# A hybrid decoder layer on one core: attention scores as 128-row contractions with parts spread by DMA, HGRN's updates and outputs as single lists, the relative bias padded to 128 rows and columns

## The chip, the cores and the metric

The kernel runs on one core of a Trainium2 chip. The metric is the time of one execution in microseconds (us). TensorE (PE) does the matrix products, and its weight loads (PEld) overlap with them; VectorE (DVE), ScalarE (ACT) and GpSimd (POOL) do the elementwise work; SyncE (SP) issues the DMAs. Each engine works through its own list of instructions in order.

## The reference, cut to what matters

One layer on x of 512 positions by 1024 channels, all in float32. One input projection (1024 to 3584 columns) feeds four branches of 256 channels each and four gates:

```
proj = x @ w_in                       # qa ka va | us | qc fc ic | qd kd vd | four gates
A: softmax(q k^T / 8 + bias) v        # 4 heads of 64, causal
B: diagonal state space (S5) and a gated linear unit
C: HGRN2: S_t = diag(f_t) S_{t-1} + (1 - f_t) outer i_t ; o_t = S_t^T q_t   # 4 heads of 64, chunks of 64
D: softmax over dilated windows       # 4 heads of 64, done as one biased causal softmax
y = concat(A, B, C, D); y = rms_norm(y) * gain * silu(gates)
x = layer_norm(ALPHA * x + y @ w_out)
```

With 512 positions all earlier keys are reachable, so A and D are both written as a full causal attention with a bias table added to the scores. The bias table (8 heads) is made on the chip from a small product, `rel_bias` against a 0/1 matrix of distances.

## The kernel before, in words

**Precision.** Most products are made of three fast ones (fp32r): a value is split into a high part `h` and a low part `l`, and `h*h + l*h + h*l` is summed in PSUM. So each projection tile of 128 rows by 512 columns takes 8 contraction steps of 3 matmuls. Some products (transposes, HGRN, S5, the product of probabilities and values) are plain fp32; the profile shows a plain fp32 product as two MATMUL instructions.

**Order.** The instruction order is not written by hand. `Order` (lines 132 to 262) is a planner: each task is a Python generator that yields instructions, or lists of PE instructions that stay together. A task has a priority (lower goes first). Projections (`projections`, priority 92) and the output product (`out_partial`, 91, `out_final`, 90) are the filler for PE; everything else goes between them when the planner's clocks say that its inputs are there, with a margin of 1 us for PE.

**Buffers.** `Tok` takes tokens and `o.rel` gives them back; a task that finds no token waits, in the planner's order. `u` stands for `NU` = 34 work tiles of 4 KB per partition. The PSUM banks are `pj` (3, projections and output product), `sc` (2, scores), `pt` (2, transposes) and `sm` (1). `raw` (4) are landing buffers of the weights, `wh` (5) the split weights. The output weights (`out_weights`) take 2 `u` tiles for each of six k steps, and ask for 6 free ones (`2 + SPARE`) before they do; the order of k is 6, 7, 4, 5, 0, 1, 2, 3. Weight loads, relays and the final stores all go through SP's one queue, in the planner's order.

**Attention before.** `evac_qk` (line 1076) copies a projected tile of two heads (head 0 in partitions 0 to 63, head 1 in 64 to 127) into `qt[name, ct][:, 0]` (high) and `[:, 1]` (low). `attn_pair` (line 1139) takes two heads and both `sc` banks, and issues six matmuls of 64 contraction rows, the two heads in turn, each in its own half of the array:

```
for j, (x, y) in enumerate(((0, 0), (1, 0), (0, 1))) for h in range(2)
```

Then `attn_head` (line 1153) adds the bias from `TB` and takes the row maximum (DVE), the exponential (ACT), transposes the probabilities (PE, ACT or DVE), and `attn_pv` multiplies by the values in 64-column halves of the array. There are 2 branches, query tiles i = 3, 2, 1, 0 with n = (i + 1) * 128 keys, and 2 pairs: 16 pairs. Branch A waits for the HGRN state (`START`), D for its own projections.

**HGRN before.** The chunk states (lines 1014 to 1031) come in four lists of 4 (the last of 2) products of 64 rows; after each, ACT or DVE adds the update to the running state, in order. The outputs (lines 1040 to 1065) come in two lists, each with products of 64 output columns (state times query) and then of 64 by 64 (in-chunk scores times values).

**Bias before.** `bias` (line 506) multiplies two slices of one tile of 34 rows, `relct`: 8 columns of table against 512 and then 128 columns of distances.

Of the kernel before, what the change touches and what calls it, by code (L numbers as in the profile page):

```python
# [11 lines left out]
F32 = mybir.dt.float32  # L12
# [253 lines left out]
def build(ctx: ExitStack, tc: tile.TileContext, xT, xN, w_in, w_out, ln_g, ln_b,  # L266
# [15 lines left out]
    def u(shape, nm, dt=F32):  # L282
        return up.tile(shape, dt, tag="u", name=nm)
# [104 lines left out]
    def load_feed():  # L388
        yield Wait("begun")
        for n_, p in enumerate(pieces):  # L390
            if n_ == 4:
                yield Tok(u=3)
                for nm, sh, sl, src in (("bc", [128, 4, 8, 32], None, s5bc.rearrange("p (a j c) -> p a j c", a=4, j=8)),
                                        ("cst2", None, None, consts[:, 586:874]), ("relct", [34, 648], None, relc),
                                        ("glw", [128, 1024], None, consts[:, 74:586])):
                    t = CT[nm] = u(sh, nm) if sh else cst2
                    yield Q.dma_start(t[:, 0:512] if nm == "glw" else t, src)
                    o.done(nm)
                    o.cur["chain"] = 0.0
            yield Tok(raw=1)  # L400
            raw = raws[p] = wp.tile([128, 512], F32, tag="raw", name=f"wr{p[0]}_{p[1]}", bufs=NR)
            yield Q.dma_start(raw, w_in[GROUPS.index(p[0]), :, 2 * p[1]:2 * p[1] + 2].rearrange("p k c -> p (k c)"))
            o.events["raw", p] = o.cur["chain"]
            o.cur["chain"] = 0.0
# [101 lines left out]
    def bias():  # L506

        yield Wait("us")
        yield Wait("relct")
        yield Delay(1.0)  # L510
        yield Tok(u=1)
        relct, bsb = CT["relct"], u([8, 640], "bsb")
        for a, n in ((0, 512), (512, 128)):
            yield Tok(sm=1)
            pb = ps(f"pb{a}", "sm")
            yield [T.matmul(pb[0:8, 0:n], relct[:, 640:648], relct[:, a:a + n], start=True, stop=True)]
            yield A.activation(bsb[:, a:a + n], pb[0:8, 0:n], AF.Copy)
            o.rel("sm")
        yield Q.dma_start(scr, bsb.unsqueeze(1).to_broadcast([8, NCP, 640]))
        o.rel("u", 2)  # L520
        yield Wait("hgrn levels")
        TB = gp.tile([128, 8, S], F32, tag="g", name="TB")
        for ph in range(128 // NCP):
            src_ = bass.AP(scr.tensor, 127 - NCP * ph, [[639, NCP], [NCP * 640, 8], [1, 512]])
            yield Q.dma_start(TB[NCP * ph:NCP * ph + NCP], src_)
            o.cur["chain"] = o.clk["PE"] + 1.5
        o.cur["chain"] = o.dma + 2.0
        TBq["t"] = TB
        o.done("TB")
# [366 lines left out]
    def hgrn():  # L896
# [114 lines left out]
        ic = H["ic"]  # L1011
        yield Tok(u=2)
        hst = [u([128, 4, 2, 128], f"hst{i}") for i in range(2)]
        for c2 in range(4):
            yield Tok(sc=1, pt=1)
            pu = [ps(f"pu{c2}_{q}", ("sc", "pt")[q], (128, 2, 128)) for q in range(2)]
            yield [T.matmul(pu[q][:, a], kt[64 * q:64 * q + 64, a, c2],
                            ic[64 * q:64 * q + 64, c2, 128 * a:128 * a + 128], start=True, stop=True)
                   for a in range(2) for q in range(2) if 2 * c2 + q < 7]
            for q in range(2):  # L1020
                c = 2 * c2 + q
                if c < 7:
                    h_ = hst[c // 4][:, c % 4]
                    if c == 0:
                        yield A.activation(h_, pu[q], AF.Copy)
                    else:
                        for a in range(2):
                            yield V.scalar_tensor_tensor(h_[:, a], hs[c - 1][:, a], tot[:, a, c:c + 1], pu[q][:, a],
                                                         OP.mult, OP.add)
                    hs[c] = h_  # L1030
                o.rel(("sc", "pt")[q])
        o.rel("u")
        o.done("hgrn state")
        o.rel("pT")
# [2 lines left out]
            yield G.memset(t_[64:128, :, :, 0:64], 0.0)  # L1037
        yield Tok(u=1)
        yC = u([128, 4, W], "yC")
        for tp in range(2):  # L1040
            yield Tok(sm=1)
            po = ps(f"ho{tp}", "sm", (128, 2, W))

            ops, ops2, seen = [], [], set()
            for t2 in range(2):
                c2 = 2 * tp + t2
                for a in range(2):
                    for q in range(2):
                        c = 2 * c2 + q
                        rq = slice(64 * q, 64 * q + 64)  # L1050
                        ca = slice(128 * a, 128 * a + 128)
                        if c:
                            ops.append(T.matmul(po[rq, t2, ca], qc[:, a, 64 * c:64 * c + 64], hs[c - 1][:, a],
                                                start=q not in seen, stop=False, skip_group_check=True))
                            seen.add(q)
                    for h in range(2):
                        for q in range(2):
                            c = 2 * c2 + q
                            rq = slice(64 * q, 64 * q + 64)
                            cl = slice(128 * a + 64 * h, 128 * a + 64 * h + 64)  # L1060
                            ops2.append(T.matmul(po[rq, t2, cl], st[h][rq, a, c2], ic[rq, c2, cl],
                                                 start=False, stop=(t2 == a == h == 1), skip_group_check=True))
            yield ops + ops2
            yield A.activation(yC[:, 2 * tp:2 * tp + 2], po, AF.Copy, scale=0.125)
            o.rel("sm")
        o.rel("u", 6)
        yield from norm_branch(3, yC)

# [5 lines left out]
    def evac_qk(n, sc):  # L1076
        def f(ct, po):
            yield Tok(u=1)
            t = qt[n, ct] = u([128, 2, S], f"{n}{ct}", F32R)
            yield A.activation(t[:, 0], po, AF.Copy, scale=sc)  # L1080
            yield V.scalar_tensor_tensor(t[:, 1], po, sc, t[:, 0].bitcast(F32), OP.mult, OP.subtract)
        return f

    def evac_v(n):
        def f(tp, po):
# [50 lines left out]
    HP = 6.5  # L1136
    ATT = {}

    def attn_pair(br, i, a, no):

        q_, k_ = (("qa", "ka"), ("qd", "kd"))[br]
        n = (i + 1) * 128
        yield Wait(q_, k_, "TB", *([("sc", no - 2)] if no else []))
        yield Tok(sc=2)
        o.done(("sc", no))
        sc = [ps(f"sc{i}_{4 * br + 2 * a + h}", "sc") for h in range(2)]
        qs = slice(128 * i, 128 * i + 128)
        yield [T.matmul(sc[h][:, 0:n], qt[q_, a][ROWS[h], x, qs], qt[k_, a][ROWS[h], y, 0:n], start=j == 0, stop=j == 2)
               for j, (x, y) in enumerate(((0, 0), (1, 0), (0, 1))) for h in range(2)]
        for h in range(2):  # L1150
            o.add(attn_head(br, i, 2 * a + h, no + h, sc[h]), HP + (no + h) * 0.01, f"head {br} {i} {2 * a + h}")

    def attn_head(br, i, hd, no, sc):
        v_ = ("va", "vd")[br]
        n = (i + 1) * 128
        hg = 4 * br + hd
        if no:
            yield Wait(("nl", no - 1))
        yield Tok(nl=1)
# [23 lines left out]
    def attn_pv(br, i, pairs):  # L1183

        v_ = ("va", "vd")[br]
        yield Wait(v_, *[("P", br, i, 2 * a + h) for a in pairs for h in range(2)])
        if pairs[0] == 0:
            yield Tok(sm=1)
            ATT[br, i] = ps(f"po{i}_{br}", "sm", (128, 4, 128))
            o.done(("po", br, i))  # L1190
        yield Wait(("po", br, i))
        po = ATT[br, i]
        yield [T.matmul(po[64 * h:64 * h + 64, a], vt[v_][:, kt, 128 * a + 64 * h:128 * a + 64 * h + 64],
                        ATT[br, i, 2 * a + h][:, kt], start=(kt == 0), stop=(kt == i))
               for a in pairs for kt in range(i + 1) for h in range(2)]
        o.rel("pT", 2 * len(pairs))
        o.rel("head", 2 * len(pairs))
        if pairs[-1] == 1:
            o.add(attn_norm(br, i, po), 1, f"norm {br} {i}")
            if i == TILES[-1]:  # L1200
                o.rel("u", 5)

    def attn_norm(br, i, po):
        yield Tok(sqa=1, ya=1)
# [41 lines left out]
    def attention():  # L1246
        n = 0
        for br in range(2):
            yield Wait(*(("qa", "ka", START), ("qd", "kd"))[br])
            for i in TILES:  # L1250
                for a in range(2):
                    yield Tok(head=2)
                    o.add(attn_pair(br, i, a, n), HP + n * 0.01, f"pair {br} {i} {a}")
                    n += 2


    lnt = {}
# [194 lines left out]
```

## Time and profile before

| | |
|---|---|
| median of 3 runs | 292.11 us (291.78 to 292.79) |
| profiled execution | 292.68 us, of which 290.9 us from the first to the last instruction (the span) |
| PE busy | 279.9 us (96% of the span), 1966 matmuls |
| PE weight loads | 225.8 us (78%) |
| DVE, ACT, POOL busy | 211.3, 142.6, 23.5 us (73%, 49%, 8%) |
| mean granted clock of TensorE | 0.994 of full speed |
| DMA | 31.08 MB, mean 107 GB/s |

The profile is of one execution. A busy engine is counted from the start of an instruction to its modelled end, and matmuls overlap, so the length of a stretch of PE work is read from the chain of waits (start, duration, what), whose pieces join end to end, not by adding durations of single matmuls.

### The profile page before, as it was taken

What the parts mean: (1) busy time and instruction counts of PE and PEld (TensorE: products, weight loads), DVE (VectorE), ACT (ScalarE), POOL (GpSimd) and SP (SyncE); (2) the same over time, 40 slices, a digit from 0 to 9 for tenths busy, and PEclk for the clock granted to TensorE, in tenths of its full rate; (3) what the DMA queues carried; (4) which work ended last, traced back from release to release, by engine and by line L of the source; (5) the groups of instructions that cost most, each with busy time, mean ns of one, the idle gap of its engine ahead of it and who ended that gap; (6) DMA issues with size and microseconds to landing.
All of it is one profiled execution on the core that took longest, in us unless ns stands there. A gap on an engine that the chain in (4) does not pass through costs nothing.

```text
span 290.9 us, 5251 instructions
## 1 busy us (share of the span) xinstructions
PE 279.9 (96%) x1966; PEld 225.8 (78%) x1966; DVE 211.3 (73%) x507; ACT 142.6 (49%) x281; POOL 23.5 (8%) x30
## 2 busy tenths in 40 slices
PE   7999999999999999989999999999999999999990
PEld 3678679988779977768897787777979777777890
DVE  2877999999999979479642465866768765776565
ACT  4677661325353433064588588876367753221000
POOL 1110000000000001100130010014000101020201
PEclk9999999999999999999999999999999999999997
DMA  6966435521322599922112320132512690121011
GB/s 194 310 190 207 133 110 120 154 82 44 104 74 66 132 127 114 163 89 74 36 57 85 95 94 0 48 98 73 149 34 74 208 357 16 44 101 55 20 72 72
DMA packets 18741, 31.08 MB, mean 107 GB/s; under 512 B 2426, under 2 KB 5882, under 8 KB 18716
## 3 DMA queue, kind: packets, MB, share of 16 engines
q1 hardware_dynamic: 18716, 30.76, 38.3%
q8 instruction: 15, 0.25, 0.4%
q14 instruction: 10, 0.08, 0.1%
HBM read 27.27 MB, written 2.42 MB: 102 GB/s over the span
## 4 chain that ended last, share of the span: by engine, by line
PE 84%; DMA 7%; DVE 5%; issue 1%; SPq 1%; ACT 1%; DVEq 0%; ACTq 0%
PE out L229 16%; PE pj_g L229 12%; PE po L229 4%; PE pj_vd L229 4%; PE pj_ic L229 4%; PE pj_kd L229 4%; PE pj_va L229 4%; PE pj_qc L229 4%; PE pj_qd L229 4%; PE pj_ka L229 4%; PE pj_us L229 4%; DMA wrg<-in_w_in_dram 4%; PE pt L229 3%; PE sc L229 3%; PE pj_qa L229 2%; PE y L229 2%
## 5 line engine op out<-in xcount | busy, mean ns | idle before, releaser
L229 PE MATMUL pj_g<-xh,whg 128*128 128x512 f32 x64 | 26.9, 421 | 0.0
L229 PE MATMUL pj_g<-xh,wlg 128*128 128x512 f32 x64 | 25.1, 392 | 0.0
L229 PE MATMUL pj_g<-xl,whg 128*128 128x512 f32 x64 | 25.1, 392 | 0.0
L229 ACT ACT_TABLE_LOAD x18 | 23.1, 1283 | 2.4 <-PE glu L229 1.4
L229 DVE CUSTOM_DVE_ANT_0 nl<-sc,TB 128x512 f32<-128x512 f32 (+3 forms) x32 | 14.6, 485 | 9.2 <-PE sc L229 9.1
L229 ACT ACTIVATE whg<-wrg 128x512 fp32r<-128x512 f32 x16 | 10.1, 629 | 22.6 <-PE pj_g L229 8.8
L229 PE MATMUL out<-woh,yh 128*128 128x512 f32 (+1 forms) x54 | 21.1, 391 | 0.0
L229 ACT ACTIVATE nl<-nl,nm 128x512 f32<-128x512 f32 (+3 forms) x32 | 17.8, 556 | 6.3 <-DVE nm L229 6.1
L229 PE MATMUL out<-woh,yl 128*128 128x512 f32 (+1 forms) x54 | 19.9, 368 | 0.0
L229 PE MATMUL out<-wol,yh 128*128 128x512 f32 (+1 forms) x54 | 19.8, 367 | 0.0
L229 DVE TENSOR_TENSOR wlg<-wrg,whg 128x512 fp32r<-128x512 f32 x16 | 11.0, 689 | 9.0 <-ACT whg L229 8.8
L229 POOL TENSOR_TENSOR msa<-msa,mhalf 128x4 f32<-128x4 f32 x8 | 9.0, 1122 | 100.8 <-DVE msa L229 100.8
L229 DVE COPY pT<-pt 128x512 f32<-128x512 f32 (+3 forms) x16 | 7.8, 488 | 12.1 <-PE pt L229 12.1
L229 PEld LDWEIGHTS pj_g<-xh,whg 128*128 128x128 f32 x64 | 12.0, 188 | 3.9 <-issue 1.4
L229 ACT ACTIVATE yh<-z 128x256 fp32r<-128x256 f32 (+1 forms) x12 | 5.7, 486 | 18.8 <-DVE z L229 18.8
L229 PE MATMUL pt<-ident,nl 128*128 128x128 f32 x80 | 14.3, 278 | 0.0
L229 PEld LDWEIGHTS pj_g<-xh,wlg 128*128 128x128 f32 x64 | 12.0, 188 | 2.7
L229 PEld LDWEIGHTS pj_g<-xl,whg 128*128 128x128 f32 x64 | 12.1, 189 | 1.9
L229 PEld LDWEIGHTS out<-woh,yh 128*128 128x128 f32 x54 | 10.2, 190 | 2.4 <-issue 0.8
L229 PEld LDWEIGHTS pt<-ident,nl 128*128 128x128 f32 x80 | 9.7, 140 | 3.1 <-issue 1.3
L229 PEld LDWEIGHTS out<-woh,yl 128*128 128x128 f32 x54 | 10.2, 189 | 1.8
L229 ACT ACTIVATE pT<-pt 128x512 f32<-128x512 f32 (+3 forms) x16 | 7.0, 434 | 9.1 <-PE pt L229 9.0
(312 smaller groups left out, 818.6 us busy)
## 6 DMA issues: line engine op xcount, KB each, us to landing
wrg<-in_w_in_dram SPq DMA_DIRECT2D x16, 256.0 KB, 4.9
wro<-in_w_out_dram SPq DMA_DIRECT2D x16, 256.0 KB, 2.8
xr<-in_xT_dram SPq DMA_DIRECT2D x8, 256.0 KB, 4.6
TB<-scr SPq DMA_DIRECT2D x8, 256.0 KB, 11.3
xn<-in_xN_dram SPq DMA_DIRECT2D x4, 512.0 KB, 8.2
out_dram<-xn SPq DMA_DIRECT2D x7, 256.0 KB, 2.0
raw<-in_w_in_dram SPq DMA_DIRECT2D x8, 128.0 KB, 4.6
wrus<-in_w_in_dram SPq DMA_DIRECT2D x4, 256.0 KB, 4.2
```

Of the source, the lines that this page charges most:

```text
L229: getattr(self.engines[op.eng], op.name)(*op.a, **op.k)
```

## The change

1. `relct` becomes a tile of 128 by 768 that POOL sets to zero before the 34 by 648 table is loaded into its corner; both bias products now take 128 rows and 128 columns of it.
2. HGRN's seven chunk updates are issued as one list of PE instructions into four PSUM banks (both `sc` and both `pt`), and the updates of the state follow.
3. HGRN's outputs are one list, into one `sm` and one `pt` bank: first all products of 64 output columns, then all of 64 by 64.
4. A new task `by_head` follows each evacuation of q and k. With four DMAs from tile to tile it builds, per head, a key tile that holds the 64 rows of the head twice (both with the high and the low part), and for the queries one tile in which partitions 0 to 63 hold a head's high part and 64 to 127 its low part. One score is then two matmuls of 128 rows: (q high over q low) with k high, and with k low. `attn_pair` is gone; each head issues its own two matmuls.

```diff
-                                        ("cst2", None, None, consts[:, 586:874]), ("relct", [34, 648], None, relc),
+                                        ("cst2", None, None, consts[:, 586:874]), ("relct", [128, 768], None, relc),
...
+                    if nm == "relct":
+                        yield G.memset(t, 0.0)
+                    yield Q.dma_start(t[:, 0:512] if nm == "glw" else t[0:34, 0:648] if nm == "relct" else t, src)
...
-            yield [T.matmul(pb[0:8, 0:n], relct[:, 640:648], relct[:, a:a + n], start=True, stop=True)]
+            yield [T.matmul(pb[:, 0:n], relct[:, 640:768], relct[:, a:a + n], start=True, stop=True)]
...
-        for c2 in range(4):
-            yield Tok(sc=1, pt=1)
...
+        yield Tok(sc=2, pt=2)
+        pu = [[ps(f"pu{x}_{q}", ("sc", "pt")[q], (128, 2, 2, 128)) for x in range(2)] for q in range(2)]
+        yield [T.matmul(pu[q][c2 // 2][:, c2 % 2, a], kt[64 * q:64 * q + 64, a, c2],
+                        ic[64 * q:64 * q + 64, c2, 128 * a:128 * a + 128], start=True, stop=True)
+               for c2 in range(4) for a in range(2) for q in range(2) if 2 * c2 + q < 7]
+        for c in range(7):
+            h_, p_ = hst[c // 4][:, c % 4], pu[c % 2][c // 4][:, c // 2 % 2]
+            if c == 0:
+                yield A.activation(h_, p_, AF.Copy)
+            else:
+                for a in range(2):
+                    yield V.scalar_tensor_tensor(h_[:, a], hs[c - 1][:, a], tot[:, a, c:c + 1], p_[:, a], OP.mult, OP.add)
+            hs[c] = h_
+            if c in (2, 3, 5, 6):
+                o.rel(("sc", "pt")[c % 2])
...
+        yield Tok(sm=1, pt=1)
+        pos_ = [ps(f"ho{tp}", ("sm", "pt")[tp], (128, 2, W)) for tp in range(2)]
+
+        ops, ops2 = [], []
         for tp in range(2):
...
-            yield ops + ops2
-            yield A.activation(yC[:, 2 * tp:2 * tp + 2], po, AF.Copy, scale=0.125)
-            o.rel("sm")
+        yield ops + ops2
+        for tp in range(2):
+            yield A.activation(yC[:, 2 * tp:2 * tp + 2], pos_[tp], AF.Copy, scale=0.125)
+            o.rel(("sm", "pt")[tp])
...
+            o.add(by_head(n, ct, t, n[0] == "k"), 5.5, f"by head {n} {ct}")
...
+    def by_head(n, ct, t, keys):
+        yield Tok(u=1 + keys)
+        if keys:
+            d = [u([128, 2, S], f"{n}{ct}_{h}", F32R) for h in range(2)]
+        else:
+            d = u([128, 2, S], f"{n}{ct}h", F32R)
+        last = 0.0
+        for h in range(2):
+            for x in range(2):
+                c = o.cur["chain"]
+                if keys:
+                    yield Q.dma_start(d[h][ROWS[x]].bitcast(F32), t[ROWS[h]].bitcast(F32))
+                else:
+                    yield Q.dma_start(d[ROWS[x], h].bitcast(F32), t[ROWS[h], x].bitcast(F32))
+                o.cur["chain"], last = c, o.cur["chain"]
+        o.cur["chain"] = last
+        qt[n, ct] = d
+        o.rel("u")
+        o.done((n, ct))
...
-    def attn_pair(br, i, a, no):
...
-        yield [T.matmul(sc[h][:, 0:n], qt[q_, a][ROWS[h], x, qs], qt[k_, a][ROWS[h], y, 0:n], start=j == 0, stop=j == 2)
-               for j, (x, y) in enumerate(((0, 0), (1, 0), (0, 1))) for h in range(2)]
...
+    def attn_head(br, i, hd, no):
...
+        yield Wait((q_, a), (k_, a), "TB", *([("sc", no - 1)] if no else []))
+        yield Tok(sc=1)
+        o.done(("sc", no))
+        sc = ps(f"sc{i}_{hg}", "sc")
+        yield [T.matmul(sc[:, 0:n], qt[q_, a][:, h, 128 * i:128 * i + 128], qt[k_, a][h][:, x, 0:n], start=x == 0, stop=x == 1)
+               for x in range(2)]
...
             if i == TILES[-1]:
-                o.rel("u", 5)
+                o.rel("u", 7)
...
-                for a in range(2):
-                    yield Tok(head=2)
-                    o.add(attn_pair(br, i, a, n), HP + n * 0.01, f"pair {br} {i} {a}")
-                    n += 2
+                for hd in range(4):
+                    yield Tok(head=1)
+                    o.add(attn_head(br, i, hd, n), HP + n * 0.01, f"head {br} {i} {hd}")
+                    n += 1
```

## Rows read from the trace of the kernel before

**Rows 1.** The page: busy us (share of the span) and instructions of PE.

```profile
PE 279.9 (96%) x1966; PEld 225.8 (78%) x1966; DVE 211.3 (73%) x507; ACT 142.6 (49%) x281; POOL 23.5 (8%) x30
```

**Rows 2.** The page: the chain that ended last, share of the span by engine.

```profile
PE 84%; DMA 7%; DVE 5%; issue 1%; SPq 1%; ACT 1%; DVEq 0%; ACTq 0%
```

**Rows 3.** Windows: length, busy by engine (PE, PEld, DVE, ACT, POOL), clock, DMA, GB/s.

```profile
120.00:130.00 10.00, 8.69 (x48) 6.50 (x48) 5.04 (x15) 4.36 (x8) 1.04 (x2) 1.00 0.56 141
```

**Rows 4.** Chain of waits, branch D's scores: start, us, engine, tile, instructions.

```profile
216.28 0.44 PE pt L229 x4
216.72 0.89 PE sc L229 x6
...
219.68 1.44 PE pj_vd L229 x12
221.33 0.72 PE sc L229 x6
222.05 0.59 PE pt L229 x4
...
236.79 0.55 PE sc L229 x6
237.33 1.62 PE out L229 x6
...
239.28 1.39 PE out L229 x6
...
245.82 0.48 PE sc L229 x6
246.30 1.58 PE out L229 x6
```

**Rows 5.** Chain of waits, the bias, HGRN, S5 and the gated unit.

```profile
34.97 0.95 PE pb L229 x2
35.92 2.96 PE pj_qc L229 x12
...
98.90 2.75 PE pj_g L229 x12
...
104.37 0.65 PE pu L229 x8
105.02 2.95 PE pj_g L229 x12
...
133.06 2.10 PE ho L229 x44
...
143.57 2.68 PE y L229 x24
146.25 4.10 PE pj_g L229 x18
...
173.90 1.36 PE glu L229 x6
```

**Rows 6.** Timeline of ACT: evacuation of va's first half, and of kt's second.

```profile
95.62 0.60 ACT L229 ACTIVATE va<-pj_va 128x512 f32<-128x512 f32 x1 [0.81 <-PE pj_va L229]
...
102.13 0.60 ACT L229 ACTIVATE fc<-kt 128x512 f32<-128x512 f32 x1 [1.59 <-PE kt L229]
```

**Rows 7.** The page: DMA issues, count, KB each, median us to landing.

```profile
wro<-in_w_out_dram SPq DMA_DIRECT2D x16, 256.0 KB, 2.8
...
TB<-scr SPq DMA_DIRECT2D x8, 256.0 KB, 11.3
```

**Rows 8.** Timeline of DVE: second half of qd evacuated.

```profile
206.71 0.69 DVE L229 SCALAR_TENSOR_TENSOR qd<-pj_qd,qd 128x512 fp32r<-128x512 f32 x1 [0.64 <-ACT qd L229]
```

**Rows 9.** Timeline of SP's queue: output weights, LayerNorm constants.

```profile
204.84 5.25 SPq L229 DMA_DIRECT2D wro<-in_w_out_dram  x4
221.03 10.03 SPq L229 DMA_DIRECT2D wro<-in_w_out_dram  x8
231.11 0.42 SPq L229 DMA_DIRECT2D lng<-in_ln_g_dram  x1
```

More of the change, by code (lines that the diff above doesn't have):

```diff
@@ L393, in load_feed @@
                 for nm, sh, sl, src in (("bc", [128, 4, 8, 32], None, s5bc.rearrange("p (a j c) -> p a j c", a=4, j=8)),
-                                        ("cst2", None, None, consts[:, 586:874]), ("relct", [34, 648], None, relc),
+                                        ("cst2", None, None, consts[:, 586:874]), ("relct", [128, 768], None, relc),
                                         ("glw", [128, 1024], None, consts[:, 74:586])):
                     t = CT[nm] = u(sh, nm) if sh else cst2
-                    yield Q.dma_start(t[:, 0:512] if nm == "glw" else t, src)
+                    if nm == "relct":
+                        yield G.memset(t, 0.0)
+                    yield Q.dma_start(t[:, 0:512] if nm == "glw" else t[0:34, 0:648] if nm == "relct" else t, src)
                     o.done(nm)
@@ L1013, in hgrn @@
         hst = [u([128, 4, 2, 128], f"hst{i}") for i in range(2)]
-        for c2 in range(4):
-            yield Tok(sc=1, pt=1)
[L1016 to L1026, printed above, removed]
-                        for a in range(2):
[L1028 to L1031, printed above, removed]
+        yield Tok(sc=2, pt=2)
[13 more added lines that the diff above has]
+                o.rel(("sc", "pt")[c % 2])
         o.rel("u")
@@ L1039, in hgrn @@
         yC = u([128, 4, W], "yC")
+        yield Tok(sm=1, pt=1)
+        pos_ = [ps(f"ho{tp}", ("sm", "pt")[tp], (128, 2, W)) for tp in range(2)]
+        ops, ops2 = [], []
         for tp in range(2):
-            yield Tok(sm=1)
-            po = ps(f"ho{tp}", "sm", (128, 2, W))
-            ops, ops2, seen = [], [], set()
+            po, seen = pos_[tp], set()
             for t2 in range(2):
@@ L1057, in hgrn @@
                         for q in range(2):
-                            c = 2 * c2 + q
                             rq = slice(64 * q, 64 * q + 64)
@@ L1137, in build @@
     ATT = {}
-    def attn_pair(br, i, a, no):
+    def attn_head(br, i, hd, no):
         q_, k_ = (("qa", "ka"), ("qd", "kd"))[br]
[L1142 to L1147, printed above, removed]
-        yield [T.matmul(sc[h][:, 0:n], qt[q_, a][ROWS[h], x, qs], qt[k_, a][ROWS[h], y, 0:n], start=j == 0, stop=j == 2)
-               for j, (x, y) in enumerate(((0, 0), (1, 0), (0, 1))) for h in range(2)]
[L1150 to L1154, printed above, removed]
+        a, h = divmod(hd, 2)
         n = (i + 1) * 128
         hg = 4 * br + hd
+        yield Wait((q_, a), (k_, a), "TB", *([("sc", no - 1)] if no else []))
[4 more added lines that the diff above has]
+               for x in range(2)]
         if no:
@@ L1250, in attention @@
             for i in TILES:
-                for a in range(2):
-                    yield Tok(head=2)
-                    o.add(attn_pair(br, i, a, n), HP + n * 0.01, f"pair {br} {i} {a}")
-                    n += 2
+                for hd in range(4):
+                    yield Tok(head=1)
+                    o.add(attn_head(br, i, hd, n), HP + n * 0.01, f"head {br} {i} {hd}")
+                    n += 1
     lnt = {}
```

## The prediction

> **What bounds the kernel now.** I read the page's busy time first. PE works 279.9 of 290.9 us, DVE 211.3, ACT 142.6 [rows 1]. A busy PE could still be waiting inside pipelined matmuls, so the chain of waits comes next: 84% of what ended last is PE, DMA has 7% and DVE 5% [rows 2]. The DMA's share is the loading at the start and one stretch in the middle, where PE loses 1.31 of 10 us [rows 3]; the granted clock there is 1.00, so PE's speed has nothing to give back. The reader is to see one thing: the filler (projections, output product) is always there, so whatever PE time a list costs, the end pays one for one. The rest of the chain then prices a list, since its pieces join end to end.
>
> **What a list costs PE.** A run of 6 full-array fp32r matmuls of 512 columns takes 1.39 us, 12 of 256 columns 1.44 us [rows 4]: 0.232 and 0.120 each. Behind a score list the same 6 matmuls take 1.62 or 1.58 us, and 4 transposes 0.59 instead of 0.44 us [rows 4]. So a list that uses the array in halves charges the next one 0.15 to 0.23; I take 0.19. A full-array fp32r list between projections (`glu`) costs 1.36 for 6 [rows 5], with no such charge; nor does S5's full-array fp32 list `y`: the 18 matmuls behind it take 4.10, 0.228 each [rows 5].
>
> **The change part by part.** The sum is made against the profiled execution, 292.68 us (span 290.9 and 1.8 around it), which lies 0.57 above the median of 292.11; I carry the difference over to the median.
>
> *Scores.* Before, a pair's list takes 0.89, 0.72, 0.55 and 0.48 us for 512, 384, 256 and 128 keys [rows 4], together 2.64, with four charges of 0.19 3.40. There are 2 branches with 2 pairs for each key length: 4 x 3.40 = 13.6 us. After, a pair is two heads with 2 full matmuls each: 4 x 0.232 for 512 keys and 4 x 0.120 for 256. For 384 the trace has no full fp32r matmul: I take the middle, 0.176. For 128 it has transposes at 0.44 / 4 = 0.11 [rows 4] as the nearest row; I take 0.12, no quicker than 256 columns. Sum 4 x (0.232 + 0.176 + 0.120 + 0.120) = 2.59, four times 10.4. Gain 3.2 us. Bounds: at half of 0.12 for the sixteen 128-key matmuls the gain is 4.2; if every head's own list still left a charge of 0.19, 32 x 0.19 = 6.1 comes back and the part loses 2.9.
>
> The old lists do overlap the two heads: from 128 to 512 keys a list grows by 0.41 us, 0.137 per 128 keys; four full matmuls grow by 4 x (0.232 - 0.120) / 2 = 0.224 [rows 4]. So by columns alone the change loses (0.224 - 0.137) x 40 units of 128 keys = 3.5 us, and it wins because the fixed part of 16 lists (0.48 - 0.137 + 0.19 = 0.53 each, 8.5 us) goes. The Trainium skill speaks against the change here: "TensorEngine Tiling (Array Packing)", section Theoretical Speedup, says that a contraction of at most 64 rows gains up to twofold from two row tiles, which the new scores give up. The trace agrees on the overlap (0.137 against 0.224). By that rule alone the sum would be 294.7 (rival 3), by the rows with the fixed part 288.0.
>
> *Chunk updates.* A list of 8 instructions takes 0.65, and the 12 projection matmuls behind it 2.95 instead of 2.75 [rows 5]. Four lists (the fourth, of one half alone, taken as equal) cost 4 x 0.85 = 3.4. The products of the two halves run side by side, so 0.65 is 4 slots of 0.11 (y: 2.68 / 24 [rows 5]) and 0.21 fixed. One list is 16 slots: 1.76 + 0.21 + 0.20 = 2.17. Gain 1.2 us, between 0.6 (only the charges go) and 1.5. It asks for all four banks of `sc` and `pt` at once; nothing else wants `sc` before the state is finished. The state's 12 DVE additions follow one another instead of waiting for four lists; DVE's work is unchanged.
>
> *Outputs.* Two lists of 2.10 [rows 5], each of two kinds, so with two fixed parts. One list saves a charge of 0.2 and one or two fixed parts of 0.2; I take 0.4, between 0.2 and 0.6.
>
> *Bias.* The first product takes 0.95 and leaves 2.96 - 2.75 = 0.21 [rows 5]. At y's 0.112 per instruction and 128 columns, two instructions of 512 columns take 0.89 and leave nothing: 0.27. The second product saves at least its charge: together 0.5, between 0 and 0.6. The memset costs nothing while POOL (8% busy [rows 1]) is free before SP comes to the table's load; if not, SP and qc's loads behind it wait a mean POOL instruction, 23.5 / 30 = 0.8 us.
>
> Gains: 3.2 + 1.2 + 0.4 + 0.5 = 5.3 us.
>
> *Copies.* Each of the 8 tiles of q and k gets four DMAs: 32 issues at 0.42 us [rows 9] are 13.4 us of SP's queue, and 16 x 256 KB + 16 x 128 KB = 6 MB more. A copy of 256 KB lands in 2.8 us on a quiet chip and 11.3 in the crowd of bias loads [rows 7]. For branch A they are hidden behind the HGRN state. For D the late one is qd's second half: written at 207.4 [rows 8], issued in 1.7, landed in 2.8, it is there at 211.9; its heads were scored at 216.72 [rows 4]. So 4.8 us are spare, and I cost the copies at nothing; in the crowded case they are 3.7 late.
>
> *Work tiles.* Key tiles double: one more per key tile, two per branch. When va's first half is evacuated, the old order holds 33 of 34 tiles (x 8; fc, kc, qc, ic 4; in-chunk scores 2; S5's bc, U4, tr, ti, both wt, fir, three cw, three z 13; gw 1; ka, qa, va 5). Two more do not fit. So va waits for the next release, after the second transposed key: evacuated at 95.62 before, it can't start before 102.73 and ends at 103.3 [rows 6]. The gate's second half wants that `pj` bank at about 101.65, where the first twelve gate matmuls end [rows 5]. Late by 0 (if S5's coefficient tiles come free first) to 1.7; I take 1.2, because the transposes that fill in take 0.44. ACT is not held up meanwhile, since the planner puts the evacuation behind the release.
>
> Sum: 292.1 - 5.3 + 1.2 = **288.0 us**.
>
> **Rivals.**
> 1. *Work tiles run short again in D.* A's and D's doubled keys hold four tiles when the second output weight (k = 7) asks for 6 free ones, so it waits for A's end, and k = 5 falls behind into the later batch. That batch issues 8 loads in 10.03 us, 1.25 each [rows 9]; two more put the output product's second step 2.5 us late, where it is PE's only filler. For it: the count. Against it: attention fills part. 290.5 us.
> 2. *The other side: D's copies stuck in SP's queue.* SP issues 4 output-weight loads from 204.84, then nothing until 221.03, because a landing buffer has to be split first [rows 9]. If qd's copies stand behind that load, they land at 221.0 + 1.7 + 2.8 = 225.5, 8.8 us after the old score. D's heads run one behind the other, so the end moves with them once they are later than the saving made by then (3.7: all but D's half of the scores) and the output product in three banks is used up. Whole price: 292.1 + 8.8 - 3.7 + 1.2 = 298.4, slower from about 4 us of lateness on. Against it: the planner issues a copy when it thinks q is written, ahead of loads whose tiles come free only at A's end.
> 3. *The change doesn't do what it says for the scores:* every list still pays a fixed part, whether in halves or not, so that only columns count. Scores lose 3.5, the rest gains 2.1, the tiles cost 1.2: 292.1 + 3.5 - 2.1 + 1.2 = 294.7; with the charge of 0.19 left behind every head, 294.1. For it: the overlap that the rows show. Against it: `glu`, a short full list without a fixed part [rows 5]. It is the Trainium skill's rule on two row tiles ("TensorEngine Tiling (Array Packing)", Theoretical Speedup) taken alone.
>
> **How the numbers follow.** Forecast 0.69, rival 1 0.15, rival 2 0.10, rival 3 0.06. The forecast's own range is 285.8 to 290 (scores up to 1.0 better, tiles 0 to 1.7, chunk updates 0.6 to 1.5, planner's shifts). The range of 285.6 to 292.4 takes in most of rival 1 and leaves out about 0.18. A measurement of this kernel tells 0.3%, 0.9 us, from no change. Faster than 291.2: the forecast and two thirds of rival 1, 0.79. Within: 0.06. Slower than 293.0: rivals 2 and 3, 0.15.
>
> **What would show it.** Right: score lists of about 0.46 us per head at 512 keys with 1.39 behind them; one `pu` list near 2.0 us; PE's busy time down by about 5 us. Wrong: a late first score of D, with DMA as its releaser; PE gaps near 100 us with `va` evacuated after `kt`; gaps after D's first output matmuls that the split weights end. The prediction falls if PE's share drops while its work shrinks.

## The result and the profile after

The changed kernel takes 288.87 us, the median of 8 runs (287.2 to 291.1), beside 291.94 for the kernel before (8 runs). The ratio is 0.9888, with a 95% interval of 0.9856 to 0.9921: 3.3 us less (2.3 to 4.2), where 4.1 less was forecast. The profiled execution, 291.1 us, is the longest of the eight; a second profile of the same kernel (e5) shows 286.16. So single spans are not compared here to the microsecond: PE's busy time, the length of lists and the places of gaps are.

The page of the changed kernel, lines that answer to [rows 1], [rows 2] and [rows 7]:

```profile
PE 275.8 (95%) x1934; PEld 229.1 (79%) x1934; DVE 211.2 (73%) x507; ACT 140.6 (49%) x280; POOL 23.6 (8%) x31
...
PE 64%; DMA 15%; DVE 15%; issue 3%; ACT 2%; SPq 1%; DVEq 0%; ACTq 0%
...
ka<-ka SPq DMA_DIRECT2D x8, 256.0 KB, 6.0
...
kd<-kd SPq DMA_DIRECT2D x8, 256.0 KB, 4.7
```

PE's busy time fell by 4.1 us. It includes twelve matmuls of zeros (`warm`) that PE does ahead of the first projection; they took 4.19 us before and 5.30 here, so the rest of PE's work fell by 5.2. PE's share of the span went from 96% to 95% and its share of the chain from 84% to 64%. That looks like the prediction's last sign against itself, PE's share dropping while its work shrinks, and isn't that: the chain now goes back through DVE and DMA where PE was working all the same, and in e5's profile of the same kernel PE has 96% of the span and this chain:

```profile
PE 93%; DVE 5%; issue 1%; DVEq 0%
```

Idle time decides it. Windows (length, busy by engine PE, PEld, DVE, ACT, POOL, clock, DMA, GB/s) from 20 to 276 us, first of the kernel before:

```profile
20.00:276.00 256.00, 254.18 (x1845) 207.25 (x1844) 190.80 (x452) 129.69 (x257) 19.23 (x17) 1.00 0.37 100
```

then of the changed kernel, with three stretches of 10 us:

```profile
20.00:276.00 256.00, 251.75 (x1824) 211.80 (x1823) 192.85 (x459) 128.52 (x258) 19.61 (x18) 1.00 0.49 126
...
100.00:110.00 10.00, 10.00 (x71) 8.40 (x70) 7.88 (x17) 3.70 (x7) 0.00 (x0) 1.00 0.93 129
110.00:120.00 10.00, 8.83 (x43) 7.26 (x42) 10.00 (x27) 2.87 (x5) 1.04 (x2) 1.00 1.06 120
120.00:130.00 10.00, 9.34 (x48) 7.34 (x49) 7.09 (x20) 4.55 (x8) 1.04 (x2) 1.00 0.59 123
```

PE idles 4.25 us in this execution instead of 1.82. In e5's profile of the same kernel it idles 1.71: a few gaps that come in one execution and not in the next make the difference. The stretch of [rows 3] improved (8.69 busy to 9.34), and the one ahead of it lost 1.17. Most of the 1.31 us lost in [rows 3] belong to that execution too: e7 and e8, whose PE work is that of the kernel before, lose 0.22 and 0.19 there. From 100 to 110 us, where the prediction put its lateness, PE is busy without a break.

The chain of waits of the changed kernel (start, us, engine, tile, instructions), to be read beside [rows 4] and [rows 5]:

```profile
107.12 1.98 PE pu L229 x28
109.10 5.68 PE pj_g L229 x24
...
130.01 3.90 PE ho L229 x92
133.91 5.67 PE pj_g L229 x24
...
142.26 0.70 PE sc L229 x4
142.96 1.39 PE pj_g L229 x6
...
208.15 0.46 PE sc L229 x2
...
214.06 0.44 PE pt L229 x4
214.50 0.47 PE sc L229 x2
214.97 2.88 PE pj_vd L229 x24
...
238.96 0.47 PE sc L229 x4
...
244.03 0.40 PE sc L229 x4
```

A head at 512 keys now takes 0.46 us, and what follows a score list takes its plain time again: 4 transposes 0.44 (0.59 in [rows 4]), 6 projection matmuls 1.39 (1.58 to 1.62). The update list is one of 1.98, the outputs one of 3.90.

Where PE idles is in PE's timeline of the changed kernel (start, us, what, in brackets the idle time before and its releaser); the first two lines are the bias:

```profile
35.63 1.02 PE L229 MATMUL pb<-relct 128*128 128x512 f32 x2
...
39.26 0.38 PE L229 MATMUL pb<-relct 128*128 128x128 f32 x2
...
117.32 0.62 PE L229 MATMUL sc<-ka,qa0h 128*128 128x512 f32 x2
...
120.08 0.73 PE L229 MATMUL sc<-ka,qa0h 128*128 128x512 f32 x2 [1.26 <-DVE hst L229]
...
125.02 1.35 PE L229 MATMUL sc<-ka,qa1h 128*128 128x512 f32 x4 [0.58 <-DMA wrg<-in_w_in_dram]
...
213.36 0.70 PE L229 MATMUL sc<-kd,qd1h 128*128 128x512 f32 x2
...
230.20 0.49 PE L229 MATMUL out<-woh,yh 128*128 128x512 f32 x1 [0.54 <-ACT woh L229]
...
230.93 0.50 PE L229 MATMUL out<-wol,yh 128*128 128x512 f32 x1 [0.23 <-DVE wol L229]
```

The second score of A waits for the last additions to the state, DVE's line

```profile
119.16 0.86 DVE L229 SCALAR_TENSOR_TENSOR hst<-hst,tot,pu 128x128 f32<-128x128 f32 x3
```

then PE waits for a gate's weights, and then the output product for its split weights. ACT's timeline, where `va` stands against [rows 6] and the late weight shows its own releaser:

```profile
101.30 1.08 ACT L229 ACTIVATE va<-pj_va 128x512 f32<-128x512 f32 x2
...
229.52 1.31 ACT L229 ACTIVATE woh<-wro 128x512 fp32r<-128x512 f32 x2 [2.43 <-DMA wro<-in_w_out_dram]
```

And SP's queue in the changed kernel, which answers to [rows 9]:

```profile
191.11 5.59 SPq L229 DMA_DIRECT2D kd<-kd  x6
...
205.09 2.48 SPq L229 DMA_DIRECT2D qd1h<-qd  x4
207.62 24.30 SPq L229 DMA_DIRECT2D wro<-in_w_out_dram  x16
```

D's copies are out by 207.57, ahead of every output weight. The price is on the other side: all 16 weight loads come after 207.62. In the kernel before, the 4 that [rows 9] shows from 204.84 were already the second four; the first had gone out here:

```profile
187.69 9.55 SPq L229 DMA_DIRECT2D wro<-in_w_out_dram  x4
```

### The profile page after: what moved, and what is told of

It is laid out like the page before. It is cut to its first block, busy times and chain, and to the rows that moved or that the text cites. A ratio compares the mean times of both kernels' runs of the same rounds, so it can differ in the third digit from the quotient of the medians.

```text
span 289.3 us, 5247 instructions
## 1 busy us (share of the span) xinstructions
PE 275.8 (95%) x1934; PEld 229.1 (79%) x1934; DVE 211.2 (73%) x507; ACT 140.6 (49%) x280; POOL 23.6 (8%) x31
## 4 chain that ended last, share of the span: by engine, by line
PE 64%; DMA 15%; DVE 15%; issue 3%; ACT 2%; SPq 1%; DVEq 0%; ACTq 0%
PE out L229 14%; PE pj_g L229 14%; PE pj_va L229 4%; PE pj_kd L229 4%; PE pj_qd L229 4%; PE po L229 4%; DMA wrg<-in_w_in_dram 3%; PE pj_vd L229 3%; PE sc L229 3%; PE pt L229 3%; DMA wrka<-in_w_in_dram 3%; DMA wro<-in_w_out_dram 3%; DMA wrqc<-in_w_in_dram 2%; PE pj_ka L229 2%; DMA wrus<-in_w_in_dram 2%
## 5 line engine op out<-in xcount | busy, mean ns | idle before, releaser
L229 PE MATMUL pj_g<-xh,whg 128*128 128x512 f32 x64 | 26.0, 407 | 0.0
L229 PE MATMUL pt<-ident,nl 128*128 128x128 f32 x80 | 13.4, 277 | 0.0
L229 PEld LDWEIGHTS out<-wol,yh 128*128 128x128 f32 x54 | 10.2, 189 | 1.8 <-DVE wol L229 0.5
```

Of the source, the lines that this page charges most:

```text
L229: getattr(self.engines[op.eng], op.name)(*op.a, **op.k)
```

## The experiments

Each was timed in five rounds beside the kernel before on the same chip; a ratio below 1 is faster than the kernel before.

**e1, the scores alone** (part 4 of the change on the kernel before), and **e2, the lists alone** (parts 1 to 3).

> The kernel before with part 4 alone (copies, per-head scores of 128 rows). Theory: PE pays a fixed part for every list that uses the array in halves; the scores' share of PE falls from 13.6 to about 10 us, and the copies and doubled key tiles give 1 to 2.5 us back as gaps: 1 to 2.6 us faster than the kernel before (ratio 0.991 to 0.997), score lists of 0.46 us per head at 512 keys. Rival (the gain is made by the merged HGRN lists and the padded bias, the scores only trade columns for overlap): no gain or slower, ratio 1.00 to 1.01.

> The kernel before with parts 1 to 3 alone (padded bias, one list of chunk updates, one list of outputs), old scores, no copies. Theory: PE's work falls by 1.2 + 0.5 + 0.6 = 2.3 us and no gap is added: ratio about 0.992. Rival (the merged lists only move waits, since updates and outputs now wait for four banks and for the last input): same time, ratio 0.998 to 1.002, PE's shorter work given back as gaps near the state.

Measured: e1 0.9968 (0.9943 to 0.9992), 290.88 us against 291.83; e2 0.9958 (0.9933 to 0.9983), 290.58. PE's busy time was 276.9 and 277.2. Five profiles with the old scores and lists (before, e3, e4, e7, e8) have a mean of 279.4, so e1 takes some 2.5 us off PE and e2 2.2 (3.2 and 1.8 without `warm`), and only 0.9 and 1.2 reach the end. e1 lies in its theory's range; e2 lies between its theory (0.992) and its rival (0.998 at least) and bears out neither.

**e3, the copies alone**: the old scores, but the copies are issued and waited for, and each key tile has one work tile more. The copied tiles aren't read, and the keys' copies are half as large (4 MB in all).

```diff
+            o.add(by_head(n, ct, t, n[0] == "k"), 5.5, f"by head {n} {ct}")
...
+        d = u([128, 2, S], f"{n}{ct}h", F32R)
...
+                    yield Q.dma_start(d[ROWS[x], h].bitcast(F32), t[ROWS[h], h].bitcast(F32))
...
-                o.rel("u", 5)
+                o.rel("u", 7)
```

> The kernel before with the copies issued (32 DMAs, 4 MB: key copies are half as long as in the changed kernel) and one more tile held per key tile, while the scores are still the old pairs computed from the original tiles and only wait, in the planner, for the copies. It leaves nothing of the result out; the copies are just not read. Theory: PE's work is unchanged and the later va and later output weights cost gaps: 1 to 2.5 us slower, ratio 1.003 to 1.009. Rival (the copies and tiles are hidden): ratio 0.998 to 1.002.

**e4, the kernel before with two work tiles fewer**, and no copy.

```diff
-    NU = 34
+    NU = 32
```

> The kernel before with 32 work tiles in place of 34, no copies. Theory that the missing tiles are what costs, not the DMAs: va's evacuation moves from 95.6 to about 102, the output weights' loads come later, and the time grows as in the run with the copies alone, by 1 to 2 us (ratio 1.003 to 1.007). Rival (the DMA traffic and SP's queue cost, not the tiles): ratio 0.998 to 1.002.

Measured: e3 1.0090 (1.0059 to 1.0121), 294.08 us; e4 1.0085 (1.0057 to 1.0112), 294.58. e3 lies at the upper edge of its theory's range, e4 above its own (1.007). A price as large as e3's is there without a single copy: two missing tiles are enough for it, some 2.5 us, and the copies add nothing that this comparison can show. That e3's own price is the tiles' is likely, not shown: e4 lacks its two tiles from the start, e3 only from the keys on, and each has an order of its own. Against e3, the new scores themselves gain 0.9968 - 1.0090, 1.2% or 3.6 us (2.4 to 4.7). PE's timeline of e4 shows what kind of price it is:

```profile
118.52 0.50 PE L229 MATMUL pj_g<-xh,whg 128*128 128x512 f32 x1 [0.75 <-ACT g0t L229]
...
230.50 1.09 PE L229 MATMUL sc<-kd,qd 64*128 64x256 f32 x6 [1.08 <-DVE nm L229]
```

Two gaps, in the middle and in D, not the ones of the changed kernel. e3 has the second one too:

```profile
232.41 1.10 PE L229 MATMUL sc<-kd,qd 64*128 64x256 f32 x6 [1.08 <-DVE nm L229]
```

e4's profile is its shortest run (292.02 us), so its gaps show a kind of price, not the size of 2.5.

**e5, the changed kernel again**, as the partner of e6.

> The changed kernel once more, beside the runs of this call. Both theories expect the ratio found before, 0.989, within its interval (0.986 to 0.992); scores and lists together (measured alone 0.997 and 0.996) would give 0.993 if they simply added.

**e6, one tile back**: HGRN's two half-filled tiles share one, on the changed kernel. **e7**: the same on the kernel before.

```diff
-        yield Tok(u=2)
+        yield Tok(u=1)
...
-        st = [u([128, 2, 4, 64], f"st{h}") for h in range(2)]
+        st2 = u([128, 2, 2, 4, 64], "st")
+        st = [st2[:, h] for h in range(2)]
...
-        o.rel("u", 6)
+        o.rel("u", 5)
```

> The changed kernel with HGRN's two half-filled tiles of in-chunk scores put into one, which gives one work tile back from 41 us to HGRN's end. Theory (two missing tiles cost about 2.5 us): va is evacuated at about 96 again, the first output weights are loaded before 200 us, and 0.5 to 1.5 us come back: ratio to the kernel before 0.984 to 0.987. Rival (one tile is not enough, the queue shifts elsewhere): ratio 0.989, as the changed kernel.

> The kernel before with the same merging of two half-filled tiles, so 35 work tiles in effect during HGRN. Theory: the kernel before holds 33 of 34 tiles when va comes and loses nothing for want of tiles, so the time stays: ratio 0.998 to 1.002. Rival (tiles bind the kernel before as well, and any tile is worth a microsecond): ratio 0.995 to 0.998.

Measured: e5 0.9880 (0.9834 to 0.9926), 288.79 us; e6 0.9940 (0.9909 to 0.9970), 290.39; e7 1.0001 (0.9972 to 1.0031), as its theory had it: the kernel before lacks no tile. The tile did what it was to do: in e6 `va` is evacuated at 94.3 again and the first output weight issued at 186.3. The time didn't follow. PE's timeline of e6 has new gaps instead:

```profile
122.27 0.73 PE L229 MATMUL sc<-ka,qa1h 128*128 128x512 f32 x2 [1.56 <-DVE nm L229]
...
229.34 0.41 PE L229 MATMUL yt<-ident,ya 128*128 128x128 f32 x2 [2.09 <-DVE ya L229]
```

So "one tile back, the time back" falls. A tile more or less moves the planner's whole order, and each order has its own gaps of 1 to 2 us; which one comes out isn't a matter of the one tile. Why e6's order is the worse is open.

**e8, the pair's six matmuls head by head**, on the kernel before: do the halves overlap only because the heads alternate?

```diff
-               for j, (x, y) in enumerate(((0, 0), (1, 0), (0, 1))) for h in range(2)]
+               for h in range(2) for j, (x, y) in enumerate(((0, 0), (1, 0), (0, 1)))]
```

> The kernel before with the six score matmuls of a pair ordered head by head instead of in turn, so that two neighbours use the same half of the array. Theory (halves overlap only when neighbours differ, and on top of it a list has a fixed part): the columns of six matmuls of 512 add up, 6 x 0.23 = 1.4 us and 0.15 to 0.2 fixed, in place of 0.89; all scores 4 x (0.65 + 0.45 + 0.25 + 0.25) = 6.4 us more, ratio about 1.02. Rival (the halves never overlapped, the list was always bound by weight loads): lists stay at 0.89 and 0.48, ratio 1.00.

Measured: 1.0004 (0.9979 to 1.0029), 292.04 us. The theory, 1.02, fell. The chain of waits of e8:

```profile
215.52 0.90 PE sc L229 x6
216.42 1.63 PE pj_vd L229 x12
...
244.66 0.49 PE sc L229 x6
245.15 1.58 PE out L229 x6
```

0.90 and 0.49, with 1.58 behind, as in [rows 4]: three matmuls in a row on one half don't hold up the three on the other.

**e9, a list per head in halves**, on the kernel before, no copies: `attn_pair` is gone and every head issues its own three.

```diff
+        yield [T.matmul(sc[:, 0:n], qt[q_, a][ROWS[h], x, qs], qt[k_, a][ROWS[h], y, 0:n], start=j == 0, stop=j == 2)
+               for j, (x, y) in enumerate(((0, 0), (1, 0), (0, 1)))]
```

**e10, the changed kernel with two heads in one list** of four full matmuls (`attn_pair` kept).

```diff
+        yield [T.matmul(sc[h][:, 0:n], qt[q_, a][:, h, qs], qt[k_, a][h][:, x, 0:n], start=x == 0, stop=x == 1)
+               for h in range(2) for x in range(2)]
```

> The kernel before, with the per-head tasks of the changed kernel but the old half-array products: each head issues its own list of three matmuls of 64 rows; no copies, no extra tiles. Theory (a list in halves has a fixed part and two heads' lists only share the array when they stand next to each other): a list of 512 keys that stands alone takes 3 x 0.21 + 0.2 = 0.85 to 0.9 us, as much as a pair did, and leaves 0.19 behind; scores up to 13 us dearer, at least 5 where heads meet; ratio 1.015 to 1.045. Rival (the changed kernel gained because heads are scheduled one by one with one score bank each): PE's longer lists are hidden, ratio 0.99 to 1.00.

> The changed kernel with two heads per list again: four full matmuls into both score banks. Theory (PE's work is what counts and a full list has no fixed part): score lists of 0.93 us per pair at 512 keys with 1.39 behind them, PE's work as in the changed kernel, ratio to the kernel before 0.986 to 0.992. Rival (scheduling by head is the gain): slower than the changed kernel by 2 us or more, ratio 0.995 or above.

Measured: e9 1.0046 (1.0021 to 1.0071), 293.44 us; e10 0.9898 (0.9865 to 0.9930), 289.02. The chain of waits of e9:

```profile
212.55 0.89 PE sc L229 x3
213.44 0.59 PE pt L229 x4
214.03 0.89 PE sc L229 x3
214.92 1.62 PE pj_vd L229 x12
...
217.19 0.73 PE sc L229 x6
```

Three matmuls of one head take 0.89, as long as six of two heads, and the charge behind (0.59 instead of 0.44) comes with each. The total was less than expected (PE busy 281.2) because many heads still met: `x6` is two heads behind one another. And of e10:

```profile
211.98 0.93 PE sc L229 x4
212.91 1.43 PE pj_vd L229 x12
```

0.93 for two heads is twice 0.46: in full-array form the grouping neither costs nor gains, and e10's interval covers the changed kernel's ratio. What wins is the use of the whole array, not the finer lists.

**e11, probabilities times values in one list of four heads** instead of two of two, on the changed kernel: the same reasoning on the last lists in halves.

```diff
-    PVH = 2
+    PVH = 4
```

> The changed kernel with the products of probabilities and values of all four heads of a query tile in one list (PVH = 4) instead of two lists: the next place where the array is used in halves. Theory (every such list costs about 0.15 of its own and 0.19 behind it): eight lists fewer, 8 x 0.3 = 2.4 us of PE less; if no wait is added the ratio to the kernel before is about 0.98. Rival (all four buffers of transposed probabilities are held until the fourth head, so the next tile's first head waits): PE's work falls the same, gaps grow, ratio 0.988 or above.

Measured: 0.9817 (0.9788 to 0.9847), 286.91 us, the best of the runs. The page and the chain of waits of e11:

```profile
PE 272.4 (96%) x1934; PEld 228.9 (80%) x1934; DVE 210.8 (74%) x507; ACT 140.7 (49%) x280; POOL 23.9 (8%) x31
```

```profile
151.04 1.90 PE po L229 x32
152.94 1.59 PE pj_g L229 x6
```

The charge behind such a list is there too (1.59), so half as many lists cost less: 2.5 us under the mean of 274.9 that five profiles of the changed kernel and its variants (after, e5, e6, e10, e12) have, 1.9 without `warm`.

**e12, fewer copies**: ACT and DVE write the queries' tile per head directly, and the keys take three copies in place: 12 copies and 3 MB instead of 32 and 6 MB.

```diff
+            if n[0] == "q":
+                for h in range(2):
+                    yield A.activation(t[0:64, h], po[ROWS[h]], AF.Copy, scale=sc)
+                    yield V.scalar_tensor_tensor(t[64:128, h], po[ROWS[h]], sc, t[0:64, h].bitcast(F32), OP.mult, OP.subtract)
```

> The changed kernel with fewer copies: ScalarE and VectorE write the queries' high and low parts straight into the per-head tile (two instructions each instead of one, no DMA), and the key tile keeps head 0 in place (three copies instead of four). DMAs of this part fall from 32 to 12 and 6 MB to 3 MB; the tiles held to the end stay the same. Theory (the missing tiles, not the copies, cost the gaps): ratio as the changed kernel, 0.986 to 0.991. Rival (SP's queue and the traffic of the copies cost): 1 to 2 us better, 0.982 to 0.985.

Measured: 0.9838 (0.9798 to 0.9878), 287.39 us. Its middle is better than the changed kernel's and lies in the range of the rival, by which copies and SP's queue cost 1 to 2 us (0.982 to 0.985); its interval reaches into the theory's range (0.986 to 0.991) as well. On the same chip it is 1.6 us under e10 (289.02). But its order moved too: the wait of A's second score, over 1.2 us in the changed kernel, e5, e10 and e11, is gone in its profile. Whether the copies cost some 1 to 2 us or the order did it isn't settled. e11 and e12 together were not run.

## Why the prediction was right, point by point

**Scores: right.** Read from the chain, two heads take 0.93, 0.70, 0.47 and 0.40 us for 512, 384, 256 and 128 keys, four times 2.50: 10.0, where 10.4 was forecast; only the 128-key lists were quicker than the 0.48 assumed. e1 against e3 gives 3.6 us, and PE's work in e1 without `warm` 3.2, forecast 3.2. The fixed part of a list in halves, on which the sign hung, is shown by e9: half the matmuls, the same 0.89. Rival 3 is refuted by the same rows. The Trainium skill's rule on two row tiles ("TensorEngine Tiling (Array Packing)", Theoretical Speedup) holds as far as the halves go: six matmuls of 512 columns take 0.89 where six full ones take 1.39 [rows 4], a factor of 1.6 of the up to 2 that it names. It doesn't decide here, because four full matmuls do the same work in 0.93 without a charge.

**Chunk updates, outputs and bias: durations right, their worth overstated.** One update list is 1.98 with 5.68 for the 24 projections behind it (5.50 is twice 2.75 [rows 5]): 2.16, forecast 2.17. The outputs take 3.90 instead of 2 x 2.10, and leave 0.17 instead of twice 0.2: 0.5, forecast 0.4. The first bias product and the 12 projection matmuls behind it take 3.63 (35.63 to 39.26) where they took 0.95 + 2.96 = 3.91 [rows 5]: 0.28, forecast 0.27. PE's busy time in e2 agrees (2.2 less, 1.8 without `warm`, forecast 2.1). But e2 gained 1.2 us, not 2.1 (0.5 to 2.0 by its interval). Its one profile, with 291.58 us one of its longer executions, has no more idle time from 20 to 276 us than before (254.18 busy in both); it loses 1.3 us more than the kernel before in its first 20 us (16.90 busy against 18.20), about what it lies above e2's median. Where the other 0.9 of the median went stays open.

**Copies: in time, as forecast; that they cost nothing isn't shown.** Keys landed in 4.7 to 6.0 us, between the bounds of 2.8 and 11.3; the issue of D's last copies ended at 207.57, they landed 2.3 us after their issue, and the first score that reads them started at 213.36, so more than 3 us were spare, forecast 4.8. An issue took longer than the 0.42 assumed (5.59 / 6 = 0.93 for the keys, 2.48 / 4 = 0.62 for the queries). Rival 2, SP's queue, did not occur: the planner issued the copies first and the output weights last. e3 against e4 shows no price of the copies, e12 leaves one of 1 to 2 us open.

**Work tiles: the step that failed; that its size was near is luck.** `va`'s first half was held back (101.30 instead of 95.62), though not beyond the second transposed key, as the prediction counted (102.73 at the earliest), and no gap came of it: PE is busy throughout 100 to 110. The idle time came elsewhere. Before 125.02 and at 230, where rival 1's mechanism appears in small (0.54 + 0.23 instead of 2.5), it comes in this execution and not in e5, whose output weights are as late. One gap comes back in four profiles, the one before 120.08: 1.26, in e5 1.25, in e10 1.23, in e11 1.25, and none like it in the kernel before, e7 and e8. There A's second score waits for the state's last additions. It doesn't read the state; what it needs is its `sc` bank, which by the code the single update list holds until then. So two sentences of the prediction failed. "Nothing else wants `sc` before the state is finished": A's first score took the first bank at 117.32, and the second had to wait. "The state's 12 DVE additions follow one another instead of waiting for four lists": DVE is busy for all of 110 to 120, and between the additions stand S5's scans and the splits of the gate's weights, so the state's end is set by DVE's order. It takes the lists and the scores together: e2 has no such gap, e1 one of 0.18. Whether the missing tiles made the order what it is stays open (in e6, with a tile back, this gap is gone and others came). In size the term was 1.2; by the medians and PE's busy time 1.2 to 1.8 came back (below), while two tiles fewer cost the old order 2.5 us (1.7 to 3.3), more than the upper bound of 1.7.

**The sum.** Forecast -5.3 + 1.2. PE's busy time gives -4.5 (279.4 to 274.9); without `warm`, which takes 4.19 to 5.30 us from one execution to the next, the same ten profiles give -5.1 (274.8 to 269.7). So 1.2 to 1.8 of it comes back, and -3.3 is measured. The parts don't add up well: e1 and e2 together would make 0.9926, the whole is 0.9888. Their intervals nearly close that, and PE's work without `warm` does add up (3.2 and 1.8 for 5.1), so the rest is idle time; the planner's order, different in every kernel here, is its likeliest cause, but that is argued, not shown.

## What to carry to other kernels

Where PE is the bound, count the lists that use the array in halves: each cost 0.2 to 0.5 us here beyond its columns (a score list 0.34 of its own and 0.19 left to the next list; e11's eight lists fewer 1.9 to 2.5 in all), so make them full-array if the columns allow it, or merge them, as e11 did for some 2 us more (286.91 against e10's 289.02 on the same chip). A term for buffers belongs in the sum with its own run: two work tiles fewer cost the kernel before 2.5 us here, twice what the merged lists alone gained. So does a list that takes more banks: ask who else wants them until the last reader is done. And where a planner sets the order, a gap seen in one profile isn't a price: removing its cause (e6) gave another of the same size.

## What the runs showed of the hardware that was not expected

The two halves of the array take their matmuls as two streams whatever their order in the list: 0.89 us for six in turn, 0.90 head by head (e8), and 0.89 for three on one half (e9). If the fourth matmul of e8's list, the first on the other half, waited for the three ahead of it, the list would take longer than the 0.89 of three alone; so PE works through its matmuls in order only within a half. And the charge on the list behind is the same after three as after six (0.59 for 4 transposes, where a full-array list leaves 0.44).

The weight loads (PEld) point to where the fixed part lies. Around a list in halves they pause, here in the kernel before:

```profile
216.64 0.53 PEld L229 LDWEIGHTS sc<-kd,qd 64*128 64x128 f32 x6 [0.17 <-issue]
217.54 0.19 PEld L229 LDWEIGHTS pj_vd<-whvd,xh 128*128 128x128 f32 x1 [0.36 <-issue]
```

Around a full-array list of the changed kernel, with the same projection behind it, no pause is recorded:

```profile
214.23 0.30 PEld L229 LDWEIGHTS sc<-kd,qd1h 128*128 128x128 f32 x2
214.58 0.19 PEld L229 LDWEIGHTS pj_vd<-whvd,xh 128*128 128x128 f32 x1
```
